# Projection and MLA head weights split in one block and kept in DRAM, in a hybrid encoder block

## The chip, the cores and the metric

One core of a Trainium2 chip runs the whole program. The metric is the device time of one execution in microseconds; a median of several runs is given. The core has TensorE (PE, with its weight loads shown apart as PEld), VectorE (DVE), ScalarE (ACT), GpSimd (POOL), and SyncE (SP), which here issues nearly all DMAs.

## What is computed

The kernel is one layer of a streaming encoder: 2,048 tokens of width 1,024, float32. All products are wanted at float32 accuracy. Cut to what matters:

```python
n = rms_norm(h, attn_norm)
z = n @ w_in                       # columns: gq 256, gk 256, gv 512, g_low 16, g_r 512, c_q 256, c_kv 128, k_r 32
...                                # GLA: 4 heads, gated linear attention in chunks, output norm, silu(g_r) gate
q_m = rms_norm(c_q, mla_q_norm) @ mla_w_uq       # 256 -> 8 heads x 96
kv  = rms_norm(c_kv, mla_kv_norm) @ mla_w_ukv    # 128 -> 8 heads x (64 + 64)
...                                # MLA: norms and rotary part of q and k, block-causal softmax attention
h = h + concat(o_g, o_m) @ w_out
h = h + square(relu(rms_norm(h, mlp_norm) @ w_mlp_up)) @ w_mlp_down
h = h + (p @ w_ple_proj) * sigmoid(rms_norm(h, ple_norm) @ w_ple_gate + b_ple_gate)
```

## The kernel before

To get float32 accuracy from TensorE's fp32r operands, every operand x is split into hi, x rounded to fp32r, and lo = x - hi (`split`, lines 88 to 95: ACT writes hi, with the norm's gain as scale where there is one, and DVE then writes lo from the raw tile and hi). A product is three matmuls, hi by hi, hi by lo, lo by hi (`mm3`, lines 97 to 100).

The first part of the kernel (lines 546 to 719) is a loop over four blocks of 512 tokens. In each block x is normalised, transposed and split into `nT` (lines 548 to 560, one buffer), and then seven groups of columns of `w_in` are multiplied with it: X (c_q, g_low, k_r, 304 columns, line 579), Y (c_kv and 192 of gv, 320, line 642), Q and K (gq and gk, 256 each, line 677, here the weights are the stationary operand and 512 tokens move), Z (the other 320 of gv, line 694) and R0 and R1 (g_r, two of 256, line 707). The weights of a group come from `wtiles` (lines 157 to 172): for each of 8 slices of 128 rows a raw tile is loaded (`rawp`, 6 buffers of 1,280 bytes a partition; X takes three DMAs a slice, Y two, the others one), and split into a tile `w` (`wp`, 9 buffers of 2,560 bytes). Every block does that anew, 56 tiles in each.

Between the matmuls of these groups lie pieces of two other chains, handed out by `drain` and `drain_mla`. The first is the gated linear attention of the block (`gla_pieces`, lines 312 to 430; its level steps use POOL, ACT, DVE and PE in turn). The second is the MLA head work: `mla_weights` (lines 433 to 445) loads and splits one half of `mla_w_uq` and `mla_w_ukv` (six raw tiles, into `wu` and `wkv` with one buffer each); `mla_tile` (lines 447 to 514) multiplies 128 tokens with them, ACT copies q and k out of PSUM (`qn`, line 461; `kn`, line 481), POOL does the rotary part and the norm's power (lines 468 to 491), DVE scales (line 494), PE transposes (line 505), and split halves (`qko`, two buffers) go to DRAM (`qd`, `kd`, line 510; `vd`, line 484). Matmul results stand in two PSUM buffers `mm`, which ACT or DVE must empty before the third result: for R0 and R1 that is the tanh on ACT (line 715) and the gate `gs` on DVE (line 716).

The source is written in one order; the framework that builds the program then plans the order of each engine's queue ahead, by its own account of what is ready when. So a split can stand in ACT's queue ahead of a copy that is written earlier. Each engine works its queue in order, and waits at the head of it. SP's queue holds the DMA issues, which wait there for a free buffer or for data.

After the loop come MLA attention over 8 heads, the output projection, the MLP and the last gate (lines 721 to 1046).

Of the kernel before, what the change touches and what calls it, by code (L numbers as in the profile page):

```python
# [11 lines left out]
F32 = mybir.dt.float32  # L12
F32R = mybir.dt.float32r
# [9 lines left out]
P = 128  # L23
# [9 lines left out]
GH, GK, GV = 4, 64, 128  # L33
RANK = 16
TAU = 16.0
MH, NOPE, ROPE, MV = 8, 64, 32, 64
QK = NOPE + ROPE
QR, KVR = 256, 128
THETA = 10000.0

O_GQ, O_GK, O_GV, O_LOW, O_GR, O_C = 0, 256, 512, 1024, 1040, 1552
CW = QR + KVR + ROPE
NEG = -1e30
WW = 320
# [4 lines left out]
def hymba_block(ctx, tc, x, p, positions, attn_norm, w_in, gla_gate_w2, gla_gate_b,  # L49
# [5 lines left out]
    dma = nc.sync.dma_start  # L55

    x, p, out = x[0], p[0, 0], out[0]
# [21 lines left out]
    kd = dram.tile([MH, QK, 2, S], F32, name="kd")  # L79
    vd = dram.tile([MH, P, NT, VW], F32, name="vd")  # L80
    mixd = dram.tile([8, P, S], F32, name="mixd")

# [52 lines left out]
    pge = ExitStack()  # L135

    def rpool(name, bufs, st):
        return st.enter_context(tc.tile_pool(name=name, bufs=bufs, side="right", reuse_waits="tile"))

    xp = rpool("xp", 2, pge)  # L140
    nTp = rpool("nTp", 1, pge)
    wp = rpool("wp", 9, pge)
    rawp = rpool("rawp", 6, pge)
    ml = rpool("ml", 2, pge)

    def wload(srcs, n):
        raws = []
        for k in range(n):
            raw = rawp.tile([P, WW], F32, name="raw")
            o = 0  # L150
            for (c0, n_) in srcs:
                dma(out=raw[:, o:o + n_], in_=w_in[k * P:(k + 1) * P, c0:c0 + n_])
                o += n_
            raws.append(raw)
        return raws

    def wtiles(srcs, ahead=()):
        res = []
        o = sum(n_ for _, n_ in srcs)
        for k in range(8):  # L160
            if k < len(ahead):
                raw = ahead[k]
            else:
                raw = rawp.tile([P, WW], F32, name="raw")
                o = 0
                for (c0, n_) in srcs:
                    dma(out=raw[:, o:o + n_], in_=w_in[k * P:(k + 1) * P, c0:c0 + n_])
                    o += n_
            w = wp.tile([P, 2, WW], F32R, name="w")
            split(w[:, 0, :o], w[:, 1, :o], raw[:, :o], gain_a[:, k:k + 1])  # L170
            res.append((w[:, 0, :o], w[:, 1, :o]))
        return res
# [14 lines left out]
    dma(out=rows_a, in_=attn_norm[0].rearrange("(k p) -> k p", p=P))  # L187
    wx0 = wload([(O_C, QR), (O_LOW, RANK), (O_C + QR + KVR, ROPE)], 2)
    load_x(1)
# [242 lines left out]

    def mla_weights(c):
        wu = ml.tile([P, 2, 2, 384], F32R, name="wu", bufs=1)
        wk_ = ml.tile([P, 2, 512], F32R, name="wkv", bufs=1)
        for k in range(2):
            for o, n_ in ((0, 192), (192, 192)):
                raw = rawp.tile([P, WW], F32, name="raw")
                dma(out=raw[:, :n_], in_=w_uq[k * P:(k + 1) * P, c * 384 + o:c * 384 + o + n_])
                split(wu[:, 0, k, o:o + n_], wu[:, 1, k, o:o + n_], raw[:, :n_], gain_q[:, k:k + 1])  # L440
        for o in (0, 256):
            raw = rawp.tile([P, WW], F32, name="raw")
            dma(out=raw[:, :256], in_=w_ukv[:, c * 512 + o:c * 512 + o + 256])
            split(wk_[:, 0, o:o + 256], wk_[:, 1, o:o + 256], raw[:, :256], gain_kv)
        return wu, wk_
# [100 lines left out]
    for b in range(NB):  # L546
# [25 lines left out]
        for gi, gb in enumerate(rope_g):  # L572
            gbv = gb.rearrange("p (a i) -> p a i", a=2).unsqueeze(1).broadcast_to([P, 4, 2, NF])
            for ti in range(2):
# [3 lines left out]
                rt.append(t_.rearrange("p t a i -> p t (a i)"))  # L578
        wx = wtiles([(O_C, QR), (O_LOW, RANK), (O_C + QR + KVR, ROPE)], wx0 if b == 0 else ())
        XW = QR + RANK + ROPE  # L580
# [60 lines left out]
        gvs = []  # L641
        wy = wtiles([(O_C + QR, KVR), (O_GV, 192)])
        for tt in range(4):
# [23 lines left out]
        for c in range(2):  # L667
            box = {}
            mla_q.append(lambda c=c, box=box: box.update(w=mla_weights(c)))
            for tt in range(4):  # L670
                mla_q.append(lambda b=b, tt=tt, c=c, box=box, a=(cT, krr, kss, rt, rc): mla_tile(b, tt, c, box["w"], *a))


        gqk = []
        for c0, nm, sc in ((O_GQ, "gq", GK ** -0.5), (O_GK, "gk", 1.0)):
            pair = [gin.tile([P, 2, 256], F32, name=nm, bufs=2) for _ in range(2)]
            wg = wtiles([(c0, 256)])
            for j in range(2):
                ps = ps_mm()
                js = slice(j * P, (j + 1) * P)  # L680
                for k in range(8):
                    mm3(ps, (wg[k][0][:, js], wg[k][1][:, js]), nst(k, slice(0, BLK)), k == 0, k == 7)
                for u in range(2):
                    A.mul(out=pair[u][:, j], in_=ps[:, u * 256:(u + 1) * 256], mul=sc)
                drain(DQ)
                drain_mla()
            gqk.append(pair)
# [5 lines left out]

        wz = wtiles([(O_GV + 192, 320)])
        for tt in range(4):
# [10 lines left out]
        for f in range(2):  # L706
            wr = wtiles([(O_GR + f * 256, 256)])
            fs = slice(f * 256, (f + 1) * 256)
# [367 lines left out]
```

## Time and profile before

| | us |
|---|---|
| median of 3 runs (3101.26 to 3103.7) | 3103.64 |
| the profiled execution | 3101.0 |
| its span, first to last instruction | 3099.3 |
| of it the first part, blocks 0 to 3 (17.7 to 694.9) | 677.2 |

The profile is of one execution. A busy time is the time in which an engine had an instruction under way; matmuls are pipelined, so a busy PE can still have room. An idle time before an instruction is put down to what ended it, its releaser. [...]

### The profile page before, as it was taken

What the parts mean: (1) busy time and instruction counts of PE and PEld (TensorE: products, weight loads), DVE (VectorE), ACT (ScalarE), POOL (GpSimd) and SP (SyncE); (2) the same over time, 40 slices, a digit from 0 to 9 for tenths busy, and PEclk for the clock granted to TensorE, in tenths of its full rate; (3) what the DMA queues carried; (4) which work ended last, traced back from release to release, by engine and by line L of the source; (5) the groups of instructions that cost most, each with busy time, mean ns of one, the idle gap of its engine ahead of it and who ended that gap; (6) DMA issues with size and microseconds to landing.
All of it is one profiled execution on the core that took longest, in us unless ns stands there. A gap on an engine that the chain in (4) does not pass through costs nothing.

```text
span 3099.3 us, 40489 instructions
## 1 busy us (share of the span) xinstructions
PE 2969.4 (96%) x14851; PEld 2451.1 (79%) x14851; DVE 1808.7 (58%) x3253; ACT 1244.2 (40%) x2446; POOL 375.7 (12%) x680
## 2 busy tenths in 40 slices
PE   7888888988999999999999999999999999999999
PEld 6777878876777777788888888878888888888877
DVE  4777677777877787454454445464354444444453
ACT  7565655644667667432222222242232222222131
POOL 3535444451000000000000000000000000000000
PEclk9999999997999999999999999999999999999999
DMA  4535434353422320411111111113311111111111
GB/s 124 139 100 144 119 112 128 88 145 91 121 72 64 98 79 19 152 43 47 49 51 45 55 41 55 41 62 126 126 55 42 55 41 55 42 55 52 45 52 55
DMA packets 231735, 238.72 MB, mean 77 GB/s; under 512 B 27398, under 2 KB 174928, under 8 KB 231536
## 3 DMA queue, kind: packets, MB, share of 16 engines
q1 hardware_dynamic: 231216, 236.01, 26.1%
q8 instruction: 117, 1.92, 0.3%
q14 instruction: 82, 0.67, 0.1%
q0 software_dynamic: 320, 0.13, 0.0%
HBM read 185.60 MB, written 50.46 MB: 76 GB/s over the span
## 4 chain that ended last, share of the span: by engine, by line
issue 54%; PE 30%; DVE 5%; POOL 5%; ACT 4%; DMA 2%; SPq 1%; DVEq 0%; POOLq 0%; ACTq 0%
PE mm L834 5%; PE mm L98 3%; PE mm L100 3%; PE mm L99 3%; PE tp L769 2%; PE big L808 2%; PE big L810 2%; PE big L809 2%; POOL rs_y L107 2%; PE big L100 1%; PE big L98 1%; PE big L99 1%; PE big L377 1%; DMA raw<-in_w_in_dram 1%; DVE xq L370 1%
## 5 line engine op out<-in xcount | busy, mean ns | idle before, releaser
L1011 DVE TENSOR_TENSOR h<-big,h 128x1024 f32<-128x1024 f32 x256 | 313.2, 1224 | 268.9 <-PE big L100 268.9
L834 PE MATMUL mm<-ph,vv 128*66 128x512 f32 (+3 forms) x960 | 242.9, 367 | 0.7 <-DVE ph L92 0.7
L105 POOL TENSOR_SCALAR rs_v<-nss 128x1 f32<-128x1 f32 x48 | 11.9, 249 | 1873.9 <-ACT nsq L113 1867.5
L98 PE MATMUL mm<-w,nT 128*128 128x320 f32 (+2 forms) x640 | 205.2, 321 | 29.0 <-ACT qn L461 17.9
L92 DVE TENSOR_TENSOR ph<-pe,ph 128x1024 fp32r<-128x1024 f32 (+3 forms) x224 | 177.5, 799 | 49.4 <-ACT ph L91 46.8
L99 PE MATMUL mm<-w,nT 128*128 128x320 f32 (+2 forms) x640 | 199.2, 311 | 0.5
L100 PE MATMUL mm<-w,nT 128*128 128x320 f32 (+2 forms) x640 | 198.6, 310 | 0.0
L776 DVE TENSOR_REDUCE mx<-tp 128x1 f32<-128x512 f32 (+2 forms) x288 | 170.0, 608 | 14.4 <-PE tp L769 12.6
L91 ACT CAST ph<-pe 128x1024 fp32r<-128x1024 f32 (+3 forms) x224 | 156.9, 711 | 31.4 <-PE mm L834 28.0
L834 PEld LDWEIGHTS mm<-ph,vv 128*66 128x66 f32 (+1 forms) x960 | 126.5, 139 | 51.4 <-DVE ph L92 1.5
L98 PEld LDWEIGHTS mm<-w,nT 128*128 128x128 f32 x640 | 128.4, 201 | 35.3 <-ACT qn L461 19.8
L95 DVE SCALAR_TENSOR_TENSOR w<-raw,gain_a,w 128x256 fp32r<-128x256 f32 (+2 forms) x224 | 122.7, 586 | 28.8 <-ACT w L94 26.5
L769 PE MATMUL tp<-kT,qT 96*128 96x512 f32 (+2 forms) x320 | 129.0, 409 | 3.2 <-DVE mx L776 1.7
L94 ACT ACTIVATE w<-raw,gain_a 128x256 fp32r<-128x256 f32 (+2 forms) x224 | 111.1, 531 | 49.1 <-DMA raw<-in_w_in_dram 40.4
L99 PEld LDWEIGHTS mm<-w,nT 128*128 128x128 f32 x640 | 128.5, 201 | 2.0 <-DVE w L95 1.3
L100 PEld LDWEIGHTS mm<-w,nT 128*128 128x128 f32 x640 | 128.3, 200 | 0.0
L808 PE MATMUL big<-qT,kT 97*128 97x512 f32 (+1 forms) x320 | 121.2, 379 | 2.9 <-ACT qT L789 2.3
L809 PE MATMUL big<-qT,kT 96*128 96x512 f32 (+1 forms) x320 | 120.4, 376 | 0.0
L810 PE MATMUL big<-qT,kT 96*128 96x512 f32 (+1 forms) x320 | 120.1, 375 | 0.0
L815 ACT ACTIVATE pe<-big 128x1024 f32<-128x1024 f32 x96 | 98.2, 1023 | 26.0 <-PE big L810 25.9
L107 POOL TENSOR_TENSOR rs_y<-rs_v,mhalf 128x1 f32<-128x1 f32 (+2 forms) x100 | 103.1, 1033 | 7.9 <-POOL rs_v L105 0.3
L769 PEld LDWEIGHTS tp<-kT,qT 96*128 96x128 f32 x320 | 62.5, 196 | 35.5 <-DVE mx L776 13.4
(3370 smaller groups left out, 8094.3 us busy)
## 6 DMA issues: line engine op xcount, KB each, us to landing
raw<-in_w_mlp_up_dram SPq DMA_DIRECT2D x128, 256.0 KB, 2.8
raw<-in_w_mlp_down_dram SPq DMA_DIRECT2D x128, 256.0 KB, 3.1
raw<-in_w_in_dram SPq DMA_DIRECT2D x160, 128.0 KB, 2.3
qd<-qko SPq DMA_DIRECT2D x64, 192.0 KB, 2.6
kd<-qko SPq DMA_DIRECT2D x64, 192.0 KB, 2.8
kT<-kd SPq DMA_DIRECT2D x32, 384.0 KB, 7.2
qT<-qd SPq DMA_DIRECT2D x32, 384.0 KB, 4.6
vd<-vt SPq DMA_DIRECT2D x32, 260.0 KB, 3.2
```

Source lines behind the costliest of these rows:

```text
L92: V.tensor_tensor(out=lo, in0=src, in1=hi, op=ALU.subtract)
L98: T.matmul(o, lhsT=a[0], rhs=b[0], start=first, stop=False)
L99: T.matmul(o, lhsT=a[0], rhs=b[1], start=False, stop=False)
L100: T.matmul(o, lhsT=a[1], rhs=b[0], start=False, stop=last)
L107: G.tensor_tensor(out=y, in0=v, in1=mhalf[:, :shape[1]], op=ALU.pow)
L769: T.matmul(ps[:, :w_], lhsT=qT[0:QK, 0, s_ * P:(s_ + 1) * P], rhs=kT[0:QK, 0, c0:c0 + w_], start=True, stop=True)
L776: V.tensor_reduce(out=mx[:, a:a + 1], in_=ps[:, :w_], axis=AX.X, op=ALU.max)
L808: T.matmul(o, lhsT=kT[:, 0, ks], rhs=qT[:, 0, c0:], start=True, stop=False)
L809: T.matmul(o, lhsT=kT[0:QK, 0, ks], rhs=qT[0:QK, 1, c0:], start=False, stop=False)
L810: T.matmul(o, lhsT=kT[0:QK, 1, ks], rhs=qT[0:QK, 0, c0:], start=False, stop=True)
L834: T.matmul(po[0:vs.stop - vs.start, c0:], lhsT=vv[:, kb, vs], rhs=ph[:, l, e, c0:], start=(kb == 4 * jb and n_ == 0), stop=(lastk and n_ = ...
L1011: V.tensor_tensor(out=hv, in0=ps, in1=hv, op=ALU.add)
```

## The change

`wtiles` is given the block and a group number. In block 0 it loads raw weights, two slices of 128 rows to one buffer (`wraw`), splits them as before, and stores each split tile, hi and lo side by side, to a tensor `wsd` in DRAM. In blocks 1 to 3 it loads the split tile from `wsd` with one DMA and splits nothing. Raw and split tiles share one pool of 12 buffers of 2,560 bytes; `rawp` is gone. `mla_weights` does the same with `wmd`: in block 0 three wider raw loads and splits and two stores a half, later two loads a half. Matmuls are unchanged.

```diff
--- before.py
+++ after.py
@@ -78,6 +78,8 @@
     qd = dram.tile([MH, QK, 2, S], F32, name="qd")
     kd = dram.tile([MH, QK, 2, S], F32, name="kd")
     vd = dram.tile([MH, P, NT, VW], F32, name="vd")
+    wsd = dram.tile([7 * 8, P, 2 * WW], F32, name="wsd")
+    wmd = dram.tile([2, P, 2560], F32, name="wmd")
     mixd = dram.tile([8, P, S], F32, name="mixd")
 
     ident = const.tile([P, P], F32, name="ident")
@@ -139,36 +141,35 @@
 
     xp = rpool("xp", 2, pge)
     nTp = rpool("nTp", 1, pge)
-    wp = rpool("wp", 9, pge)
-    rawp = rpool("rawp", 6, pge)
+    wp = rpool("wp", 12, pge)
     ml = rpool("ml", 2, pge)
 
-    def wload(srcs, n):
-        raws = []
-        for k in range(n):
-            raw = rawp.tile([P, WW], F32, name="raw")
+    def wraw(srcs, k2):
+
+        raw = wp.tile([P, 2, WW], F32, name="raw", tag="w")
+        for j in range(2):
             o = 0
             for (c0, n_) in srcs:
-                dma(out=raw[:, o:o + n_], in_=w_in[k * P:(k + 1) * P, c0:c0 + n_])
+                dma(out=raw[:, j, o:o + n_], in_=w_in[(k2 * 2 + j) * P:(k2 * 2 + j + 1) * P, c0:c0 + n_])
                 o += n_
-            raws.append(raw)
-        return raws
-
-    def wtiles(srcs, ahead=()):
+        return raw
+
+    def wtiles(b, g, srcs, ahead=()):
+
         res = []
-        o = sum(n_ for _, n_ in srcs)
+        n = sum(n_ for _, n_ in srcs)
         for k in range(8):
-            if k < len(ahead):
-                raw = ahead[k]
+            if b == 0 and k % 2 == 0:
+                raw = ahead[k // 2] if k // 2 < len(ahead) else wraw(srcs, k // 2)
+            kept = wsd[g * 8 + k][:, :2 * n]
+            w = wp.tile([P, 2 * WW], F32R, name="w")
+            v = w[:, :2 * n].rearrange("p (l n) -> p l n", l=2)
+            if b == 0:
+                split(v[:, 0], v[:, 1], raw[:, k % 2, :n], gain_a[:, k:k + 1])
+                dma(out=kept, in_=w[:, :2 * n].bitcast(F32))
             else:
-                raw = rawp.tile([P, WW], F32, name="raw")
-                o = 0
-                for (c0, n_) in srcs:
-                    dma(out=raw[:, o:o + n_], in_=w_in[k * P:(k + 1) * P, c0:c0 + n_])
-                    o += n_
-            w = wp.tile([P, 2, WW], F32R, name="w")
-            split(w[:, 0, :o], w[:, 1, :o], raw[:, :o], gain_a[:, k:k + 1])
-            res.append((w[:, 0, :o], w[:, 1, :o]))
+                dma(out=w[:, :2 * n].bitcast(F32), in_=kept)
+            res.append((v[:, 0], v[:, 1]))
         return res
 
     def tmp(shape, nm):
@@ -185,7 +186,8 @@
     load_x(0)
     rows_a = tmp([8, P], "rows_a")
     dma(out=rows_a, in_=attn_norm[0].rearrange("(k p) -> k p", p=P))
-    wx0 = wload([(O_C, QR), (O_LOW, RANK), (O_C + QR + KVR, ROPE)], 2)
+    WX = [(O_C, QR), (O_LOW, RANK), (O_C + QR + KVR, ROPE)]
+    wx0 = [wraw(WX, 0)]
     load_x(1)
     rows = tmp([4, P], "rows")
     G.dma_start(out=rows[0:2], in_=mla_q_norm[0].rearrange("(k p) -> k p", p=P))
@@ -430,18 +432,24 @@
         return [diagonal] + lv[:DP] + [decays] + lv[DP:] + [lambda c=c: chunk(c) for c in range(2)]
 
 
-    def mla_weights(c):
+    def mla_weights(b, c):
         wu = ml.tile([P, 2, 2, 384], F32R, name="wu", bufs=1)
         wk_ = ml.tile([P, 2, 512], F32R, name="wkv", bufs=1)
-        for k in range(2):
-            for o, n_ in ((0, 192), (192, 192)):
-                raw = rawp.tile([P, WW], F32, name="raw")
-                dma(out=raw[:, :n_], in_=w_uq[k * P:(k + 1) * P, c * 384 + o:c * 384 + o + n_])
-                split(wu[:, 0, k, o:o + n_], wu[:, 1, k, o:o + n_], raw[:, :n_], gain_q[:, k:k + 1])
-        for o in (0, 256):
-            raw = rawp.tile([P, WW], F32, name="raw")
-            dma(out=raw[:, :256], in_=w_ukv[:, c * 512 + o:c * 512 + o + 256])
-            split(wk_[:, 0, o:o + 256], wk_[:, 1, o:o + 256], raw[:, :256], gain_kv)
+        flat = [wu.rearrange("p l k n -> p (l k n)").bitcast(F32), wk_.rearrange("p l n -> p (l n)").bitcast(F32)]
+        kept = [wmd[c][:, 0:1536], wmd[c][:, 1536:2560]]
+        if b == 0:
+            for k in range(2):
+                raw = wp.tile([P, 2 * WW], F32, name="raw", tag="w")[:, :384]
+                dma(out=raw, in_=w_uq[k * P:(k + 1) * P, c * 384:(c + 1) * 384])
+                split(wu[:, 0, k], wu[:, 1, k], raw, gain_q[:, k:k + 1])
+            raw = wp.tile([P, 2 * WW], F32, name="raw", tag="w")[:, :512]
+            dma(out=raw, in_=w_ukv[:, c * 512:(c + 1) * 512])
+            split(wk_[:, 0], wk_[:, 1], raw, gain_kv)
+            for f, k in zip(flat, kept):
+                dma(out=k, in_=f)
+        else:
+            for f, k in zip(flat, kept):
+                dma(out=f, in_=k)
         return wu, wk_
 
     def mla_tile(b, tt, c, wts, cT, krr, kss, rt, rc):
@@ -576,7 +584,7 @@
                 G.tensor_tensor(out=t_, in0=cst[:, bs_, ti].unsqueeze(2).broadcast_to([P, 4, 2, NF]),
                                 in1=gbv, op=ALU.mult)
                 rt.append(t_.rearrange("p t a i -> p t (a i)"))
-        wx = wtiles([(O_C, QR), (O_LOW, RANK), (O_C + QR + KVR, ROPE)], wx0 if b == 0 else ())
+        wx = wtiles(b, 0, WX, wx0 if b == 0 else ())
         XW = QR + RANK + ROPE
         cT = ml.tile([P, 2, 3, BLK], F32R, name="cT", bufs=1)
         lowT = gin.tile([RANK + 1, BLK], F32, name="lowT", bufs=1)
@@ -639,7 +647,7 @@
             level_masks()
 
         gvs = []
-        wy = wtiles([(O_C + QR, KVR), (O_GV, 192)])
+        wy = wtiles(b, 1, [(O_C + QR, KVR), (O_GV, 192)])
         for tt in range(4):
             if tt % 2 == 0:
                 gvs.append(gin.tile([P, 2, GH * GV], F32, name="gv"))
@@ -666,15 +674,15 @@
         V.tensor_tensor(out=rc[:, 1].rearrange("p a t -> p (a t)"), in0=r, in1=r, op=ALU.mult)
         for c in range(2):
             box = {}
-            mla_q.append(lambda c=c, box=box: box.update(w=mla_weights(c)))
+            mla_q.append(lambda b=b, c=c, box=box: box.update(w=mla_weights(b, c)))
             for tt in range(4):
                 mla_q.append(lambda b=b, tt=tt, c=c, box=box, a=(cT, krr, kss, rt, rc): mla_tile(b, tt, c, box["w"], *a))
 
 
         gqk = []
-        for c0, nm, sc in ((O_GQ, "gq", GK ** -0.5), (O_GK, "gk", 1.0)):
+        for g, c0, nm, sc in ((2, O_GQ, "gq", GK ** -0.5), (3, O_GK, "gk", 1.0)):
             pair = [gin.tile([P, 2, 256], F32, name=nm, bufs=2) for _ in range(2)]
-            wg = wtiles([(c0, 256)])
+            wg = wtiles(b, g, [(c0, 256)])
             for j in range(2):
                 ps = ps_mm()
                 js = slice(j * P, (j + 1) * P)
@@ -691,7 +699,7 @@
             pend += gla_pieces(u, b * BLK + u * 256, gqk[0][u], gqk[1][u], bts[u], gvs, gss)
 
 
-        wz = wtiles([(O_GV + 192, 320)])
+        wz = wtiles(b, 4, [(O_GV + 192, 320)])
         for tt in range(4):
             ts_ = slice(tt * P, (tt + 1) * P)
             ps = ps_mm()
@@ -704,7 +712,7 @@
 
         gss.extend(gin.tile([P, 2, GH * GV], F32, name="gs", bufs=GSB) for _ in range(2))
         for f in range(2):
-            wr = wtiles([(O_GR + f * 256, 256)])
+            wr = wtiles(b, 5 + f, [(O_GR + f * 256, 256)])
             fs = slice(f * 256, (f + 1) * 256)
             for tt in range(4):
                 ts_ = slice(tt * P, (tt + 1) * P)
```

## Rows read from the trace of the kernel before

**Rows 1.** Busy time of the engines over the whole span, from the page.

```profile
PE 2969.4 (96%) x14851; PEld 2451.1 (79%) x14851; DVE 1808.7 (58%) x3253; ACT 1244.2 (40%) x2446; POOL 375.7 (12%) x680
```

**Rows 2.** Busy by stretch: stretch, length, busy of five engines, clock, DMA share, GB/s.

```profile
17.70:169.80 152.10, 133.39 (x825) 120.84 (x824) 101.95 (x236) 94.49 (x234) 67.92 (x135) 0.96 0.46 128
...
344.40:521.20 176.80, 155.02 (x1016) 140.96 (x1016) 128.13 (x284) 104.55 (x277) 79.71 (x142) 0.95 0.43 119
```

**Rows 3.** Waits of PE, blocks 1 to 3: us in total, times, longest.

```profile
PE mm L98 <- ACT qn L461: 13.7, 6, 3.8
PE tp L505 <- DVE qn L494: 9.3, 6, 2.5
PE mm L98 <- ACT nT L91: 8.4, 3, 3.3
PE mm L98 <- DVE gs L716: 6.5, 9, 1.5
```

**Rows 4.** Timeline at the start of R0, block 2: start, us, what, idle before.

```profile
476.70 0.51 ACT L94 ACTIVATE w<-raw,gain_a 128x256 fp32r<-128x256 f32 x1 [4.87 <-DMA raw<-in_w_in_dram]
...
477.49 0.47 ACT L461 COPY qn<-mm 128x384 f32<-128x384 f32 x1
...
478.01 0.58 PE L98 MATMUL mm<-w,nT 128*128 128x256 f32 x1 [3.79 <-ACT qn L461]
```

**Rows 5.** Timeline at the start of block 2, ACT and PE.

```profile
343.36 0.55 ACT L94 ACTIVATE w<-raw,gain_a 128x304 fp32r<-128x304 f32 x1 [1.62 <-DMA raw<-in_w_in_dram]
343.81 1.05 ACT L91 CAST nT<-tp 128x512 fp32r<-128x512 f32 x2
...
344.43 0.62 PE L98 MATMUL mm<-w,nT 128*128 128x304 f32 x1 [3.28 <-ACT nT L91]
```

**Rows 6.** Timeline within R0 of block 2, DVE and PE.

```profile
497.14 1.67 DVE L95 SCALAR_TENSOR_TENSOR w<-raw,gain_a,w 128x256 fp32r<-128x256 f32 x4
...
499.20 0.50 PE L98 MATMUL mm<-wkv,cT 128*128 128x512 f32 x1 [1.51 <-DVE gs L716]
```

**Rows 7.** Splits of projection weights, from the page's groups: busy, mean ns, idle before.

```profile
L95 DVE SCALAR_TENSOR_TENSOR w<-raw,gain_a,w 128x256 fp32r<-128x256 f32 (+2 forms) x224 | 122.7, 586 | 28.8 <-ACT w L94 26.5
...
L94 ACT ACTIVATE w<-raw,gain_a 128x256 fp32r<-128x256 f32 (+2 forms) x224 | 111.1, 531 | 49.1 <-DMA raw<-in_w_in_dram 40.4
```

**Rows 8.** Waits of PE at the start of R0, blocks 1 and 3.

```profile
PE mm L98 <- ACT qn L461: 2.8, 1, 2.8
...
PE mm L98 <- ACT qn L461: 2.7, 1, 2.7
```

**Rows 9.** Waits of DVE, blocks 1 to 3.

```profile
DVE qn L494 <- POOL rn L490: 45.8, 24, 3.0
```

**Rows 10.** Busy by stretch, five stretches at the lower clock: the first, and the sum.

```profile
302.40:305.80 3.40, 3.40 (x19) 3.40 (x18) 1.85 (x5) 0.83 (x3) 3.15 (x7) 0.50 0.64 179
...
sum 20.80, PE 20.73 PEld 20.67 DVE 14.07 ACT 10.16 POOL 11.41; mean PE 4.15 PEld 4.13 DVE 2.81 ACT 2.03 POOL 2.28
```

**Rows 11.** DMA issues: count, KB each, us to landing; and one line's durations in ns.

```profile
raw<-in_w_mlp_up_dram SPq DMA_DIRECT2D x128, 256.0 KB, 2.8
...
raw<-in_w_in_dram SPq DMA_DIRECT2D x160, 128.0 KB, 2.3
...
L167 SPq DMA_DIRECT2D raw<-in_w_in_dram x314: 327/382/1822, 5.1 to 672.7; - x157
```

**Rows 12.** Busy by stretch: 256-column matmuls at full clock.

```profile
483.30:488.00 4.70, 4.70 (x39) 4.64 (x38) 2.79 (x8) 1.29 (x3) 1.63 (x2) 1.00 0.26 69
```

**Rows 13.** Waits of PE in block 0.

```profile
PE mm L98 <- ACT qn L461: 4.5, 3, 2.8
```

**Rows 14.** Timeline in block 1, POOL and DVE.

```profile
253.91 1.29 POOL L339 TENSOR_TENSOR qe<-gq,eb 128x512 f32<-128x512 f32 x1
...
253.99 1.63 DVE L494 TENSOR_TENSOR qn<-qn,rn 128x384 f32<-128x384 f32 x1 [1.95 <-POOL rn L490]
```

**Rows 15.** Durations of one line, ns, shortest, median, longest.

```profile
L494 DVE TENSOR_TENSOR qn<-qn,rn x32: 557/794/1627, 83.2 to 680.0; 128x384 f32<-128x384 f32 x32
```

## Prediction

> **What bounds the kernel now.** First the page's busy table: PE is busy for 2969.4 of the span of 3099.3 us [rows 1]. Since matmuls are pipelined that is no proof that PE runs full, so I went to the stretch that the change touches. The rest of the kernel (attention, output projection, MLP, gate) issues the same work as before, and starts when this stretch has ended. I cut the stretch by the four blocks of 512 tokens with the busy-by-stretch view: block 2 takes 176.8 us with PE busy 155.0, DVE 128.1, ACT 104.6, POOL 79.7 [rows 2]. No engine is full for a whole block, so what counts is who holds PE up. The view of waits for PE in blocks 1 to 3 names it: 13.7 us for ACT's copy of qn out of PSUM, 9.3 us for DVE's scaling of qn, 8.4 us for ACT's cast of nT, 6.5 us for DVE's gate gs [rows 3].
>
> Then the timelines at those waits, to see what ACT or DVE did just before. At the start of group R0 (first output-gate group) PE idles 3.79 us before its first matmul at 478.01. ACT meanwhile stood at a weight split, from about 471.8 to 476.70, because its raw tile had not landed (4.87 us idle, ended by that DMA). The qn copy that PE needs stood behind that split in ACT's queue and ran at 477.49 [rows 4]. At the start of block 2 the same: a split that waits for its raw tile runs at 343.36, the nT cast behind it at 343.81, and PE at 344.43 [rows 5]. In the second MLA tile of R0, four splits take 1.67 us on DVE from 497.14, ahead of the gs that frees PE's PSUM bank, and PE waits 1.51 us [rows 6]. So in this stretch PE waits mostly for the order in the ACT and DVE queues, and weight splits stand at the head of it.
>
> **The change, part by part.**
>
> *Splits removed in blocks 1 to 3.* 3 x 56 of the 224 splits of projection weights go: 168/224 of 122.7 us is 92 us of DVE, and 168/224 of 111.1 us is 83 us of ACT [rows 7]; the MLA weight splits of three blocks go too. Most of this was beside PE work and is worth nothing by itself. What is on the path is the waits above:
> - R0 starts: 2.8, 3.8 and 2.7 us in blocks 1, 2 and 3, 9.3 us in all, part of the 13.7 [rows 3, 8]. Without the split ACT copies qn during PE's own transposes, so all 9.3 go.
> - Block starts: 8.4 us in three times [rows 3]. The casts themselves remain, and I keep 0.5 us each for them: 6.9 go.
> - gs: 6.5 us in nine times, of which the three of R1's kind are about 1.5 each [rows 3, 6]. I take 4 (between 0 and 6.5).
> - The other 4.4 of the 13.7 are the starts of group Z (rest of gv). There PE afterwards meets the wait for the scaling of qn, which ends when POOL ends: DVE waits 45.8 us for POOL's rn in these blocks [rows 3, 9]. PE would only arrive there earlier and wait longer. I take 0 (between 0 and 4.4).
> [...]
>
> Sum: 9.3 + 6.9 + 4 + 9 = 29.2 us.
>
> *Loads of kept weights.* A tile of two halves is 256 KB at 256 columns, twice the raw tile. A 256 KB weight load of the MLP lands after 2.8 us, a 128 KB one after 2.3 us [rows 11], so a load costs 0.5 us more, but no ACT and DVE step follows it. The ring of 12 buffers holds a group's 8 tiles and 4 of the next; the first four loads are issued a group ahead, the last four wait until PE has let go of tiles 0 to 3 of the group before. With 256 columns a matmul takes 0.12 us at full clock (39 in 4.70 us) [rows 12], and that happens 21 to 12 matmuls before the group ends, 2.5 to 1.4 us; the loads land 0.3 to 1.4 us after the group's end, and tile 4 is needed 12 matmuls, 1.4 us, into the next one. That is nearly even. This is the new wait, on SP: behind such a load stand the stores of qd, kd and vd, for which ACT's next cast into the two qko buffers waits. The trace of before doesn't show it; the bounds are 0 and 2 us for each of 21 groups (the 2.8 us of a whole landing less the margin). I take 0.3, nearer to 0, since PE often has MLA matmuls and transposes between two groups: +6 us. Loads of the second half's MLA weights wait for the first half's last tile; their first user comes after two more sets of Z's matmuls, 48 of them: nothing, unless SP is held up, then a landing of 2.8 us a block.
>
> *Block 0.* It splits as before and adds 60 stores of 18.7 MB. An issue takes 0.38 us of SP [rows 11], 23 us in all if none of it is hidden; and DMA engines, busy 0.46 at 128 GB/s in block 0 [rows 2], carry 123 GB/s more in its 152 us, which at today's share per byte would put them near 0.9. A store waits on SP for DVE's second half; behind it stand raw loads and the stores of qd, kd, vd. Against that, raw tiles now come two to a buffer, so four free buffers hold all eight raw tiles of the next group where six held six: the late seventh load of R0 goes here too, most of the 4.5 us of waits for qn in this block [rows 13]. I set +4 for the stores (between 0 and 23, nearer 0 because a group's raw loads are wanted some 20 us after they are issued) and -4 for the loads: 0. SBUF use is equal: 12 tiles of 2,560 bytes against 9 of these and 6 of 1,280.
>
> *Total.* -29 + 6 + 0 = -23 us. The profiled execution took 3101.0 us (1.7 over its span), which is 2.6 below the median of 3103.64; so 3078 for such an execution, about **3080** for the median.
>
> [...] DVE's scaling of qn took 1.63 us from 253.99, while POOL's qe, which reads SBUF, ran from 253.91 for 1.29 us [rows 14]; at its shortest it takes 0.557 [rows 15]. [...]
>
> **The rivals.**
> [...]
> [...]
> 3. *Slower: loads too late in blocks 1 to 3.* The last four loads of each group wait for PE, and then take a whole landing. If each group loses 2 us, that is 42 - 29 = +13, 3117. It decides from 29.2/21 = 1.4 us a group on. For it: the margin worked out above is close to nil. Against: four of eight tiles are there before.
> 4. *Slower: block 0 in series.* If SP's order puts the two stores of a pair of tiles ahead of the next raw pair, each pair costs landing 2.3, first ACT half 0.5, two DVE halves 1.2 and two issues 0.8, 4.8 us [rows 7, 11], of which PE covers 0.8; three such pairs, less a lead of 3 us from the group before, are 9 us for each of 7 groups: +63 - 23, 3144. It outweighs the gain from 23/7 = 3.3 us a group on.
>
> That the weights are split anew after all is excluded: in blocks 1 to 3 no split is issued.
>
> **How the numbers follow.** Forecast 0.52, rival 1 0.13, rival 2 0.12, rival 3 0.14, rival 4 0.09. The forecast's own range is 3066 to 3094. The range for 8 in 10 runs from 3053 to 3114. Below rival 1 it has the rest of gs (2.5), a block 0 without cost for its stores (4) and 4 for waits on the 175 us of ACT and DVE work that I gave nothing; above, it ends short of rival 3's price, so that rival 4 and the worse half of rival 3 are left out. About 0.2%, 6 us, is what a measurement can tell from no change. Faster 0.66 (forecast, rival 1, a little of rival 2), same 0.12, slower 0.22.
>
> **What would show it.** [...] PE waits for DMA of w would show rival 3, ACT's splits in block 0 waiting for raw tiles rival 4. I am wrong if blocks 1 to 3 don't get shorter although the splits are gone: then POOL or the loads set their length.

## The result and the profile after

The changed kernel takes 3122.25 us, the kernel before 3102.45 us on the same chip: a ratio of 1.0067 with a 95% interval of 1.0050 to 1.0085. It is 0.67% slower; the forecast was 3080 us, faster by about 0.75%, and the time lies above the range's upper end of 3114.

The page of the kernel after begins as follows (busy time, share of the span and instructions of each engine; the last line is from the part on DMA queues).

```profile
span 3120.1 us, 39698 instructions
...
PE 2981.5 (96%) x14851; PEld 2453.4 (79%) x14851; DVE 1710.6 (55%) x3043; ACT 1158.1 (37%) x2236; POOL 368.5 (12%) x680
...
HBM read 213.72 MB, written 69.21 MB: 91 GB/s over the span
```

The work that was to go is gone: DVE falls from 1808.7 to 1710.6 us and ACT from 1244.2 to 1158.1 [rows 1], by 98 and 86, where 92 and 83 were forecast for the projections' splits and some more for those of the MLA weights. The time is 20 us longer all the same. PE's busy time, for the same 14851 matmuls, is 12.1 us longer too; by the estimates below a lower clock makes some 8.5 of that, 13.7 more in block 0 and 5.2 less in blocks 1 to 3.

The next view is busy time by stretch for blocks 0, 1 and 2, cut at the first X matmul of each block: stretch, its length, busy of PE, PEld, DVE, ACT and POOL, granted clock, DMA share, GB/s.

```profile
16.10:210.60 194.50, 153.53 (x824) 129.74 (x823) 99.78 (x228) 93.22 (x226) 67.64 (x136) 0.87 0.65 202
210.60:378.80 168.20, 151.75 (x1016) 137.77 (x1016) 96.33 (x215) 76.03 (x209) 77.76 (x141) 0.98 0.61 188
378.80:546.10 167.30, 152.56 (x1017) 138.73 (x1016) 96.81 (x216) 76.21 (x209) 77.80 (x142) 0.97 0.57 177
```

Against [rows 2], block 2 falls from 176.8 to 167.3 us, and block 0 rises from 152.1 to 194.5, at a granted clock of 0.87 instead of 0.96. The granted clock is the share of TensorE's full clock that the trace records; every record in the traces of both kernels is 1.00 or 0.50, and a stretch has their mean. The lengths of the four blocks in every kernel of this study (block 3 to the end of its last R1 matmul), with the whole time as a median and its ratio to runs of the kernel before on the same chip (medians 3099.8 to 3102.45 us):

| kernel | block 0 | 1 | 2 | 3 | time, us | ratio to before [95%] |
|---|---|---|---|---|---|---|
| before | 152.2 | 174.6 | 176.8 | 168.7 | 3102.45 | |
| after | 194.5 | 168.2 | 167.3 | 164.5 | 3122.25 | 1.0067 [1.0050, 1.0085] |
| e1_store_act | 185.1 | 169.4 | 167.5 | 164.9 | 3112.9 | 1.0050 [1.0034, 1.0067] |
| e2_ring_only | 158.7 | 173.6 | 178.2 | 171.6 | 3104.27 | 1.0012 [1.0001, 1.0022] |
| e3_store_only | 167.3 | 175.6 | 174.1 | 168.1 | 3111.85 | 1.0041 [1.0028, 1.0054] |
| e4_own_raw9 | 175.4 | 168.7 | 167.3 | 166.8 | 3105.08 | 1.0021 [1.0010, 1.0031] |
| e5_raws_first | 157.2 | 167.4 | 167.8 | 163.4 | 3082.23 | 0.9942 [0.9928, 0.9957] |
| e6_next_raws_first | 159.7 | 169.5 | 170.2 | 164.2 | 3086.25 | 0.9950 [0.9933, 0.9967] |
| e7_next_two_first | 155.7 | 164.4 | 168.1 | 163.7 | 3076.76 | 0.9925 [0.9906, 0.9945] |
| e8_two_again | 155.6 | 164.8 | 170.0 | 162.6 | 3078.73 | 0.9932 [0.9920, 0.9944] |
| e9_x_three | 163.9 | 164.3 | 174.3 | 164.8 | 3096.17 | 0.9987 [0.9978, 0.9996] |
| e10_mla_split | 150.4 | 167.1 | 171.2 | 161.3 | 3075.28 | 0.9926 [0.9912, 0.9940] |

The lengths are those of one profiled execution each. That of e2 was the longest of its eight (3110.75 us) and that of e6 the longest of its four (3093.88), so a few us in a length can be chance.

The sum is plain. Blocks 1 to 3 take 500.0 us instead of 520.1: 20.1 us less, where 23 were forecast. Block 0 takes 42.3 us more, where nothing was forecast. 42.3 - 20.1 = 22.2, against 20.8 that the span grew.

**Who holds PE up in block 0.** The waits of PE, of ACT and of SP's DMA queue in block 0 of the kernel after (who waited for whom: us in total, times, longest):

```profile
PE mm L100 <- ACT w L96: 12.8, 11, 3.5
PE mm L100 <- DVE vt L97: 5.4, 4, 1.8
PE tp L513 <- DVE qn L502: 5.4, 2, 3.5
PE mm L101 <- DVE w L97: 4.7, 4, 3.7
```

```profile
ACT w L96 <- DMA raw<-in_w_in_dram: 28.9, 15, 3.7
```

```profile
SPq L169 <- DVE w L97: 50.9, 29, 4.2
```

PE waits for both halves of the split, ACT's (L96, 12.8 us) and DVE's (L97, 4.7). ACT's half waits 28.9 us for raw tiles. In the kernel before that wait was this:

```profile
ACT w L94 <- DMA raw<-in_w_in_dram: 8.7, 5, 3.8
```

And SP stands 50.9 us at L169, the store of a split tile, waiting for DVE's half. In the kernel before it waited for DVE too, but less, and at the raw load itself (L167), for a buffer:

```profile
SPq L167 <- DVE w L95: 36.9, 22, 10.2
```

Why a store makes raw tiles late is seen at the start of R0, in the timelines of SP, ACT, DVE and PE from 162.8 us (start, length, what, idle before):

```profile
162.80 0.48 SPq L153 DMA_DIRECT2D raw<-in_w_in_dram  x1
163.37 0.88 SPq L169 DMA_DIRECT2D wsd<-w  x2
164.30 0.49 SPq L153 DMA_DIRECT2D raw<-in_w_in_dram  x1
164.84 0.45 SPq L518 DMA_DIRECT2D kd<-qko  x1
166.30 0.32 SPq L169 DMA_DIRECT2D wsd<-w  x1
166.72 0.88 SPq L153 DMA_DIRECT2D raw<-in_w_in_dram  x2
```

```profile
165.25 0.51 ACT L96 ACTIVATE w<-raw,gain_a 128x256 fp32r<-128x256 f32 x1 [3.33 <-DMA raw<-in_w_in_dram]
...
169.30 0.91 ACT L96 ACTIVATE w<-raw,gain_a 128x256 fp32r<-128x256 f32 x2 [1.47 <-DMA raw<-in_w_in_dram]
```

```profile
165.79 0.48 DVE L97 SCALAR_TENSOR_TENSOR w<-raw,gain_a,w 128x256 fp32r<-128x256 f32 x1 [3.35 <-ACT w L96]
```

```profile
165.81 0.51 PE L100 MATMUL mm<-w,nT 128*128 128x256 f32 x2 [1.22 <-ACT w L96]
```

Raw loads and stores take turns. The slice issued at 162.80 lets ACT split at 165.25, for which ACT sat idle 3.33 us and PE 1.22. DVE's half follows at 165.79, and only then, at 166.30, can SP issue the store that it stood at. The next pair of raw slices, behind that store, is issued at 166.72, and ACT splits it at 169.30, idle again until it lands. So from a raw load to the load behind its store it is 3.9 us here, one step after the other.

PE can't fill all of that, and falls to the low clock besides. These are the sums over the stretches of block 0 at a granted clock of 0.50, before and after:

```profile
sum 13.60, PE 12.90 PEld 12.86 DVE 7.66 ACT 6.92 POOL 3.60; mean PE 4.30 PEld 4.29 DVE 2.55 ACT 2.31 POOL 1.20
```

```profile
sum 51.10, PE 40.35 PEld 33.35 DVE 27.57 ACT 19.70 POOL 15.79; mean PE 5.04 PEld 4.17 DVE 3.45 ACT 2.46 POOL 1.97
```

By the view by stretch PE sits idle 41.0 us in block 0, where it was 18.7: 22.3 us of the 42.3. The other 20.1 are busy time, though the matmuls are the same. In the kernel after K's 512-column matmuls follow one another by 0.43 us at 0.50 (from 102.57 us) and by 0.23 at 1.00 (from 107.56). So (40.35 - 12.90) / 2, some 14 us, is clock, as an estimate; what makes up the other 6 isn't shown.

**Blocks 1 to 3.** The waits of PE in the kernel after, to be held against [rows 3]:

```profile
PE tp L513 <- DVE qn L502: 9.9, 7, 2.8
PE tp L566 <- DVE xt L119: 7.0, 3, 2.7
PE mm L100 <- DVE gs L724: 6.3, 11, 1.5
PE big L379 <- DVE dl L374: 5.9, 6, 1.5
...
PE mm L100 <- DMA w<-wsd: 0.5, 1, 0.5
```

The first and third waits of [rows 3], 13.7 us for ACT's copy of qn and 8.4 for ACT's cast of nT, are gone. The wait for the scaling of qn stays (9.3 to 9.9), so does that for gs (6.5 to 6.3), the loads of kept weights cost 0.5, and a wait for the next block's x tile has grown to 7.0 us. At the start of block 2, where PE had waited behind a split [rows 5], the nT cast now runs ahead of PE (timeline, as above):

```profile
378.20 1.07 ACT L93 CAST nT<-tp 128x512 fp32r<-128x512 f32 x2
378.83 0.41 PE L100 MATMUL mm<-w,nT 128*128 128x304 f32 x1
```

### The profile page after: what moved, and what is told of

The parts are those of the page before. It is cut to its first block, busy times and chain, and to the rows that moved or that the text cites. A ratio compares the mean times of both kernels' runs of the same rounds, so it can differ in the third digit from the quotient of the medians.

```text
span 3120.1 us, 39698 instructions
## 1 busy us (share of the span) xinstructions
PE 2981.5 (96%) x14851; PEld 2453.4 (79%) x14851; DVE 1710.6 (55%) x3043; ACT 1158.1 (37%) x2236; POOL 368.5 (12%) x680
## 4 chain that ended last, share of the span: by engine, by line
issue 54%; PE 29%; DVE 5%; POOL 5%; ACT 4%; DMA 3%; SPq 0%; POOLq 0%; ACTq 0%; DVEq 0%
PE mm L842 5%; PE mm L100 3%; PE mm L102 3%; PE mm L101 3%; PE tp L777 2%; POOL rs_y L109 2%; PE big L816 2%; PE big L817 2%; PE big L818 2%; PE big L102 1%; PE big L100 1%; PE big L101 1%; DMA xt<-in_x_dram 1%; PE big L379 1%; ACT ph L93 1%
## 5 line engine op out<-in xcount | busy, mean ns | idle before, releaser
L107 POOL TENSOR_SCALAR rs_v<-nss 128x1 f32<-128x1 f32 x48 | 11.4, 237 | 1878.2 <-ACT nsq L115 1877.4
L100 PE MATMUL mm<-w,nT 128*128 128x320 f32 (+2 forms) x640 | 205.1, 325 | 17.3 <-ACT w L96 12.8
L829 ACT ACTIVATE pe<-big 128x512 f32<-128x512 f32 (+3 forms) x128 | 54.9, 437 | 77.6 <-DVE big L828 77.6
L379 PE MATMUL big<-xq,dl 128*128 128x128 f32 x448 | 63.4, 280 | 15.0 <-DVE dl L374 9.5
```

The costliest lines, as they stand in the source:

```text
L100: T.matmul(o, lhsT=a[0], rhs=b[0], start=first, stop=False)
```

## The experiments

Several theories stood for block 0's 42 us. Theory A is rival 4 of the prediction: the stores stand in SP's queue ahead of the raw loads, and each waits for its tile's split. Against it: the shared ring alone (rival B below: raw tiles now come in twos and take turns with split tiles), the 18.7 MB of stores as traffic (rival C), or the loads of kept weights. Except where it is said, each kernel computes all that the reference asks.

**e1: the stores in ACT's queue.** The kernel after with

```diff
-                dma(out=kept, in_=w[:, :2 * n].bitcast(F32))
+                A.dma_start(out=kept, in_=w[:, :2 * n].bitcast(F32))
...
-                dma(out=k, in_=f)
+                A.dma_start(out=k, in_=f)
```

> The changed kernel, with the 60 stores of split tiles issued from ACT's queue instead of SP's; nothing else moved, same bytes, same shared ring. In the changed kernel block 0 takes 194.5 us against 152.1 before (42 more), and blocks 1 to 3 are together about 20 us shorter. Theory A (order on SP: the store of a tile waits on SP for DVE's half, and the next raw loads stand behind it): raw loads run ahead again, block 0 near 155 (152 plus the issues on ACT), the whole near 3082. Rival B (the shared ring: a raw tile gets its buffer only in turn with the split tiles): block 0 stays near 194, the whole near 3122. Rival C (the traffic: 18.7 MB of stores slow the loads): block 0 near 194 as well, raw loads landing later than 2.5 us.

Block 0 took 185.1 us, not some 155, and the whole 3112.9: 9 us of 42 came back. My expectation was missed, though not because the order doesn't matter. ACT's waits in block 0 show where the store's wait went:

```profile
ACT w L96 <- DVE w L97: 7.8, 5, 2.8
ACT w L96 <- DMA raw<-in_w_in_dram: 6.3, 6, 3.5
ACT gk L692 <- DMA wsd<-w: 5.1, 1, 5.1
...
ACT qsq L468 <- DVE w L97: 4.5, 2, 2.4
```

The wait for raw tiles fell from 28.9 to 6.3 us, so SP's queue had made them late. But ACT doesn't use DVE's half of a split for the next split (L96) or for qsq (L468), and yet waits for it. It is the store in its queue that waits for it, and holds up the work behind, as here in ACT's timeline (the 5.1 us before gk are put down to a store's landing, and are another matter):

```profile
113.72 0.33 ACTq L169 DMA_DIRECT2D wsd<-w  x1
114.09 0.49 ACT L468 ACTIVATE qsq<-mm 128x384 f32<-128x384 f32 x1 [2.10 <-DVE w L97]
```

In both runs the store waited in the queue that issued it: 50.9 us on SP in the kernel after, and in e1 the 7.8 and 4.5 us that ACT waited for DVE's half. So another queue moved the wait, it didn't remove it, and e1 alone could not tell A from the rest.

**e2: the ring alone.** Raw tiles in twos in the ring of 12, as after, but nothing is kept; each block splits.

```diff
-            if b == 0 and k % 2 == 0:
+            if k % 2 == 0:
...
-            if b == 0:
-                split(v[:, 0], v[:, 1], raw[:, k % 2, :n], gain_a[:, k:k + 1])
-                dma(out=kept, in_=w[:, :2 * n].bitcast(F32))
-            else:
-                dma(out=w[:, :2 * n].bitcast(F32), in_=kept)
+            split(v[:, 0], v[:, 1], raw[:, k % 2, :n], gain_a[:, k:k + 1])
```

> Raw and split tiles in one ring of 12 as in the changed kernel, two slices to a raw buffer, the wider MLA raw loads, but every block splits its weights and nothing is stored or loaded back. Theory A (order of stores on SP) and rival C (traffic): near the kernel before, 3095 to 3107, blocks near 152 and 175 us. Rival B (the ring): each of the four blocks some 40 us longer, near 3260.

**e3: the stores alone.** The kernel before, with its own buffers for raw and split tiles, and block 0's stores added, which nobody reads.

```diff
-            w = wp.tile([P, 2, WW], F32R, name="w")
-            split(w[:, 0, :o], w[:, 1, :o], raw[:, :o], gain_a[:, k:k + 1])
+            wt = wp.tile([P, 2 * WW], F32R, name="w")
+            w = wt[:, :2 * o].rearrange("p (l n) -> p l n", l=2)
+            split(w[:, 0], w[:, 1], raw[:, :o], gain_a[:, k:k + 1])
+            if b == 0:
+                dma(out=wsd[g * 8 + k][:, :2 * o], in_=wt[:, :2 * o].bitcast(F32))
```

> The kernel before with its own two pools (9 split, 6 raw buffers), plus the 56 stores of split projection weights in block 0 from SP's queue; nobody reads them, all blocks split. Theory A: the stores stand on SP, but raw tiles have buffers of their own and can be issued before them, so block 0 is between 155 and 175, the whole 3106 to 3126. Rival B: block 0 near 152, the whole near 3104. Rival C: block 0 near 194, the whole near 3145.

Block 0 of e2, then of e3, in the view by stretch (columns as above):

```profile
16.50:175.20 158.70, 138.99 (x823) 124.29 (x822) 97.88 (x229) 91.30 (x228) 69.28 (x135) 0.92 0.45 125
```

```profile
17.40:184.70 167.30, 141.93 (x822) 126.53 (x822) 98.41 (x231) 93.50 (x233) 68.52 (x137) 0.91 0.68 211
```

Neither alone makes up the 42.3 us: the ring costs 6.5 us here (its execution was a long one; by the medians the whole kernel is 4 us longer than before) and the stores 15.1. Even with the four MLA stores, which e3 lacks and for which e10 below gives some 5 us, the sum is well short: each makes the other worse. So rival B alone is out, and so is rival C, which expected 194 us of e3. e2 says one more thing. Its blocks 1 to 3 (173.6, 178.2, 171.6) are no shorter than those of before, although raw slices there come in twos too; so the 20 us that the kernel after gains there don't come from the ring, but from the splits that are gone.

**e4: buffers of their own.** The kernel after with 9 buffers for split tiles and 3 pairs for raw tiles, the same SBUF.

```diff
-    wp = rpool("wp", 12, pge)
+    wp = rpool("wp", 9, pge)
+    rawp = rpool("rawp", 3, pge)
...
-        raw = wp.tile([P, 2, WW], F32, name="raw", tag="w")
+        raw = rawp.tile([P, 2, WW], F32, name="raw")
```

> The changed kernel with the same SBUF cut in two pools: 9 split tiles and 3 raw pairs. Stores stay on SP. Block 0: theory A expects 160 to 180 (the planned order has six raw loads ahead of the first stores, later ones mixed), rival B near 152, rival C near 194. Blocks 1 to 3 have one load ahead instead of four: if late loads matter (the third rival of the prediction) each grows by 7 groups times 1 to 2 us, from 168 to 175 to 182; if not they stay near 168.

Block 0 took 175.4 us: half of the loss went with the shared ring, 23 us stayed with the stores. It also tries rival 3 of the prediction, since with 9 buffers only one load of the next group can go ahead. PE's waits in blocks 1 to 3:

```profile
PE mm L100 <- DMA w<-wsd: 4.4, 12, 0.7
```

Even so the loads cost 4.4 us in 12 times, and the three blocks take 502.8 us against 500.0. Rival 3 is out: it wanted 2 us in each of 21 groups.

**e5: source order alone.** The kernel after, with the same ring, queue, stores and bytes; in block 0 a group now asks for its four raw pairs first, then splits eight times, then stores eight times.

```diff
+        if b == 0:
+            raws = early.pop(g, list(ahead))
+            while len(raws) < 4:
+                raws.append(wraw(srcs, len(raws)))
...
-                dma(out=kept, in_=w[:, :2 * n].bitcast(F32))
+                puts.append((kept, w[:, :2 * n].bitcast(F32)))
...
+        if b == 0 and g < 6:
+            early[g + 1] = [wraw(SRCS[g + 1], k2) for k2 in range(AHEAD0)]
+        for o_, i_ in puts:
+            dma(out=o_, in_=i_)
```

AHEAD0 is 0 here; SRCS lists the columns of each group.

> The changed kernel with one thing reordered in block 0's source: all four raw pairs of a group are loaded ahead of its eight splits, and its eight stores come after them. Same ring of 12, same queue (SP), same stores and bytes. In the planned order of SP's queue the stores of a group now stand in one row behind its raw loads, where they stood in ones and twos between them. Earlier runs: block 0 took 152 us before, 159 with the ring alone, 167 with the stores alone beside pools of their own, 185 with the stores on ACT's queue, 194 as changed. Theory A (each raw pair waits behind the stores of the pair before): block 0 near 160 (the 159 of the ring and a few us of issues), the whole near 3085. Rival C (the traffic of the stores, or the ring with the stores' hold on its buffers): block 0 at 185 to 194, the whole 3110 to 3120.

This settles that the order of the source is the cause. Block 0 takes 157.2 us and the whole 3082.23, faster than before (0.9942). Block 0 by stretch, ACT's wait for raw tiles there, and SP's timeline:

```profile
16.80:174.00 157.20, 134.68 (x824) 117.92 (x822) 96.08 (x227) 88.14 (x222) 69.28 (x135) 0.96 0.77 246
```

```profile
ACT w L96 <- DMA raw<-in_w_in_dram: 5.9, 2, 5.0
```

```profile
80.06 4.86 SPq L183 DMA_DIRECT2D wsd<-w  x8
84.97 1.82 SPq L153 DMA_DIRECT2D raw<-in_w_in_dram  x3
...
93.08 2.70 SPq L153 DMA_DIRECT2D raw<-in_w_in_dram  x5
```

Eight stores go out in 4.86 us, with raw loads in rows of three and five behind them instead of in twos between. ACT's wait for raw tiles falls from 28.9 to 5.9 us, and the granted clock is 0.96 again. The same bytes pass, in less time: DMA engines are busy 0.77 at 246 GB/s, against 0.65 at 202 in the kernel after. So the traffic is not what made block 0 long. e5 changes the turns in the ring and the order on SP together; what each of them is worth is seen only from e2, e3 and e4.

**e6, e7, e8: raw pairs of the next group ahead of the stores.** e5 with AHEAD0 = 3 (e6) and 2 (e7, and e8 the same again).

```diff
-    AHEAD0 = 0
+    AHEAD0 = 2
```

> As the run before, and in addition three of the four raw pairs of the next group are loaded ahead of a group's stores. Theory A: no raw load but the last pair can stand behind a wait of its own group's stores; block 0 near 156, the whole near 3080, lower than the run before by 2 to 6 us. If the stores standing in one row cost nothing further, both are equal. Rival C: as the run before, 3110 to 3120.

> As the run before with two raw pairs of the next group ahead of the stores instead of three, which leaves two buffers of the ring free for the MLA raw tiles and for the first splits. Theory A: within 4 us of the other two, 3080 to 3088; if the ring is too tight with three, this one is the faster.

> The kernel of the seventh run once more, with more rounds, as the base of the next two and to fix its ratio: 0.9925 was measured with few runs. Expected 3074 to 3083, ratio 0.990 to 0.995. [...]

With three pairs neither block 0 (159.7 against 157.2 us) nor the whole (3086.25 against 3082.23) is shorter than e5's, against what I expected; with two it is 155.7 and 155.6, within 4 us of the kernel before, and the whole takes 3076.76 and 3078.73, 0.68% less than before by e8, which has more executions. Why two should beat three isn't settled: the intervals of e5, e6 and e7 overlap.

**e9: a third x tile.** The wait for the x tile, grown in blocks 1 to 3, is seen at the start of block 2 in the kernel after (timeline, with the idle time before and what ended it):

```profile
378.63 0.33 SPq L183 DMA_DIRECT2D xt<-in_x_dram  x1
...
384.49 1.06 ACT L115 ACTIVATE nsq<-xt 128x1024 bf16<-128x1024 f32 x1 [2.89 <-DMA xt<-in_x_dram]
...
387.48 1.06 PE L566 MATMUL tp<-ident,xt 128*128 128x128 f32 x8 [2.67 <-DVE xt L119]
```

There are two x buffers. The tile's load is issued when PE has let go of a buffer, at 378.63; ACT waits 2.89 us for it to land, at 384.49, and PE waits 2.67 us until DVE has normalised the tile. e9 is e7 with a third, paid for with one buffer of the ring.

```diff
-    xp = rpool("xp", 2, pge)
+    xp = rpool("xp", 3, pge)
...
-    wp = rpool("wp", 12, pge)
+    wp = rpool("wp", 11, pge)
```

> The same with a third buffer for the x tiles and 11 instead of 12 in the ring (the SBUF holds no more). In the changed kernel PE arrives earlier at the third x tile of a block than that tile does: its load is issued when the first tile's buffer comes free, and PE waits 7.0 us in three times in blocks 1 to 3, where it waited 2.0 before; that is what came late next behind the removed splits. If so, these waits shrink below 1 us each, and the whole by 4 to 9 us against the run before. If the tile is late for another reason (POOL's norm), nothing changes; if the ring's twelfth buffer matters, it gets slower by up to 5.

In blocks 1 to 3 the x waits vanished (5.6 us in e8), yet the kernel is 17 us slower than e8, where at most 5 had been expected. PE's waits of e9 in these blocks show some of what took their place (in e8 they were 8.5 us for qn and 2.7 for loads of kept weights):

```profile
PE tp L524 <- DVE qn L513: 12.1, 7, 2.1
...
PE mm L100 <- DMA w<-wsd: 4.8, 7, 1.4
...
PE tp L577 <- DVE nT L94: 3.1, 2, 1.5
```

and in block 0 (163.9 us instead of 155.6) PE waits for ACT's split again (0.9 us in e8):

```profile
PE mm L100 <- ACT w L96: 5.6, 3, 4.2
```

The two changes weren't tried apart. These waits for splits and loads make it likely that the buffer missing from the ring costs more than the x tile gave; what a third x tile gives beside a ring of 12 isn't known.

**e10: the MLA weights split in every block.** e7 without the part of the change on the MLA heads' weights.

```diff
-        if b == 0:
+        if True:
...
-            for f, k in zip(flat, kept):
-                dma(out=k, in_=f)
-        else:
-            for f, k in zip(flat, kept):
-                dma(out=f, in_=k)
```

> The first kernel of this call with one part undone: the MLA weights are split in every block, not kept (four stores and the loads of three blocks go). If the MLA part gives its share by engine time (16 us of DVE and 17 of ACT in three blocks against 92 and 83 for the projections), some 15% of the gain of 20 us, the whole gets 3 us slower; if these splits stood ahead of nothing that PE waits for, it is equal within 2 us.

3075.28 us, 0.9926 [0.9912, 0.9940], against e8's 0.9932 [0.9920, 0.9944]: no difference that can be told, and no sign of the 3 us that the MLA part was to give. So the gain comes from the input projections, as far as these runs can tell. The two lengths that moved most are block 0 (150.4 from 155.6, without the MLA stores) and block 1 (167.1 from 164.8, with splits again).

## Why the prediction was wrong

**The step that failed** is the term for block 0, put as "+4 for the stores and -4 for the loads: 0". It measured +42.3. The -4 is borne out, with PE's waits for ACT's copy of qn in block 0 down from 4.5 us [rows 13] to 0.8; the +4 is not. The reason I gave for it, that "a group's raw loads are wanted some 20 us after they are issued", held for a part of the tiles only, even before. With loads and splits of block 0 matched in their order, ACT's half began between 1.9 and 23.5 us after the load was issued, 15 us or more for 15 of the 56 tiles and at most 6.1 for half of them. After the change none has more than 11.4 us, and half have at most 4.1. e3 shows that stores put into SP's order, each waiting for DVE, already cost 15 us where raw tiles have buffers of their own, and e2 to e5 that they cost 42 where raw pairs get their buffers in turns with split tiles, in source order. I had written that mechanism down as rival 4, with SP's order as its condition, and gave it 0.09. The range left it out. The short leads stood in the trace of before. I asked what the resources allow (free buffers, SP's 23 us of issues, DMA share near 0.9), and not what order the source asks for: in the loop of wtiles a pair's two stores stand ahead of the next raw pair. Which of the planner's choices turns this into SP's order is argued from the timelines, not shown apart.

Rival 4's price was 63 us in block 0, made of 4.8 us a pair. In the timeline above such a turn took 3.9. The sum was too high all the same: 42.3 / 7 is 6.0 us a group, not 9. Of that, part is clock, some 14 us of the 42.3 by the estimate above, a term that rival 4 had left out; so by that estimate its pairs held PE up for less than half of what it reckoned.

**Blocks 1 to 3** were right in sum, -20.1 against -23, and that is partly luck, since the terms were off both ways. The view by stretch, before and after, splits the sum into idle and busy time of PE:

```profile
169.80:689.90 520.10, 460.19 (x3038) 418.48 (x3039) 382.30 (x839) 308.70 (x816) 235.50 (x415) 0.96 0.42 118
```

```profile
210.60:710.60 500.00, 454.60 (x3040) 413.41 (x3041) 288.05 (x640) 225.52 (x618) 228.76 (x414) 0.98 0.57 177
```

Idle time fell by 14.5 us, busy time by 5.6. Term by term:
- *Splits off ACT's queue.* R0 starts and block starts: 16.2 forecast, the waits for qn (13.7) and nT (8.4) are gone. Right, and low: Z's 4.4, put at nothing, went as well, and the wait for the qn scaling, which was to take them over, grew only from 9.3 to 9.9.
- *gs.* 4 us forecast, 0.2 found (6.5 to 6.3). In [rows 6] DVE runs splits ahead of gs, but without them PE waits for gs as long; what sets its end now wasn't looked into.
- *Clock.* No run shows the 9 us that stand for it as the last term of the 29.2; some 5 were found. PE was busy for 33.7 us at a granted clock of 0.50 in these blocks, and for 23.2 after; half of the difference is 5.2, as an estimate. The five stretches of [rows 10] were 20.7 us of the 33.7. None is left at a start of R0 or of a block, but other stretches grew from 12.9 to 23.2 us, behind waits that stayed or came.
- *Loads.* 6 us forecast, 0.5 found, although the loads land later than I took from [rows 11]. These are the DMA issues of the kernel after (form, count, KB each, median us from issue to landing):

```profile
w<-wsd SPq DMA_DIRECT2D x96, 256.0 KB, 4.2
w<-wsd SPq DMA_DIRECT2D x48, 320.0 KB, 5.1
```

  Taken from the MLP's loads, 2.8 us was too short by 1.4 for the same 256 KB. The margin I had worked out would have been overrun by that, so the working was wrong twice. That PE's MLA matmuls and transposes between the groups cover more than I gave them is the likely reason, and isn't shown. e4, with three loads less ahead, has 4.4 us of waits.
- *Not foreseen.* The x tile's wait, 2.0 to 7.0 us. The blocks got shorter around a chain that the change doesn't touch.

**The other rivals.** Rival 1, that POOL and DVE run freer, is not borne out: POOL's busy time in block 2 fell from 79.7 to 77.8 us, PE's wait for the qn scaling did not shrink (9.3 to 9.9), and that scaling's median of 794 ns [rows 15] is 796 in the kernel after. Fewer splits made POOL and DVE's scaling little faster, if at all. Rival 2, that waits come back elsewhere, is true in part: 22 us of waits went and PE's idle time fell by 14.5, so some 8 came back, of which 6 are named (x tile +5.0, qn +0.6, loads 0.5). Rival 3 is out by 0.5 us and by e4.

With block 0 in a better order (e5 to e8) the kernel takes 3077 to 3086 us, where the forecast of 3080 stood. The gain of the kept weights was judged about right in size; that the change as written pays for it in block 0 was not seen. Of the versions that ran, e5 to e10 beat both kernels, e7 (and e8, the same source) and e10 by the most.

## What to carry to other kernels

In these runs a store that waited for its producer held up whatever was queued behind it (SP stood 50.9 us at such stores in block 0 of the kernel after): before adding one, write out its queue's order in the loop, and ask which load stands behind it and who needs that load next. If the load feeds the producer of the next store, the two run in series, as here at 3.9 us a turn; then issue the loads of the whole group first and the stores together afterwards, which cost 3 to 5 us of block 0 here instead of 42, while another queue brought back 9 of the 42 and made that queue's engine wait. A buffer ring shared by what is loaded and what is made from it tied the two as well: buffers of their own took 19 us off block 0 in e4. And when one wait is taken away, look for the chain beside it that is late next, as the x tile was (2.0 to 7.0 us).

## What the runs showed of the hardware

- 18.7 MB of stores in some 157 us, with the DMA engines busy 0.77 at 246 GB/s, lengthened block 0 by 3 to 5 us once they were in order (e5, e8); the same bytes in the order of the kernel after cost 42.
- The same 256 KB from DRAM landed after 4.2 us with the DMA engines busy about 0.6 (kept weights, blocks 1 to 3), and after 2.8 us in the MLP of the kernel before [rows 11]. Whether the traffic or the layout makes the difference isn't shown.
- In block 0 late weights cost about double their waits: PE's idle time grew by 22.3 us and the block by 42.3. PE was busy at a granted clock of 0.50 for 40.4 us there, against 12.9 before, and some 14 us are lost by that, by the estimate above.
- Matmuls overlap: in the kernel before each of the 256-column matmuls from 484.30 us on is listed with 0.28 us, and the next starts 0.12 us after it.
- ACT worked its queue in order: at the start of R0 in block 2 of the kernel before, the last matmul for the copy of qn ended at 472.9 us, and the copy ran only at 477.49, behind the split that waited for its raw tile until 476.70 [rows 4].
